# A five-engine scan of a gated delta-rule layer: the scheduler's order of four queues replaced by the written one

## Chip, cores, metric

One core of one Trainium2 chip runs the whole layer in one launch. The time is the device time of that core in microseconds; lower is better. The kernel before was timed three times.

## What is computed

One layer over 2048 latent tokens and 256 context tokens, width 1024, float32. A layer-normed, modulated input is projected to all branches at once. Branch A is a chunked gated delta rule (8 heads of 128) that runs over the tokens in both directions; branch B is a gated short convolution. Both are projected, merged by sigmoid gates, projected again and added to the input in front of a last layer norm. The core of branch A, for each head and direction, is

```
m     = tril(k_beta @ k.T * decay, -1)
t_inv = inverse(eye + m)
u, w  = t_inv @ v_beta, t_inv @ (k_beta * exp(g_cum))
qk    = (q @ k.T) * decay
v_new = u - w @ s
o     = (q * exp(g_cum)) @ s + qk @ v_new
s     = s * d + (k * exp(g_last - g_cum)).T @ v_new
```

The outputs of both directions are added, RMS-normed by head, gated, and go through `w_a`.

## The kernel before

The work has three stages. First the projections (a Strassen scheme of 512-column products, each operand split into a high and a low part). Then the scan. Then the last product with `w_out` and the layer norm.

**The scan** (function `window`, from L1164) goes over 18 chunks of 128 tokens in two directions. The directions alternate, so there are 36 visits. It is a software pipeline: iteration `i` of the loop works on four visits at once, called `v0` to `v3`.

- `v3`, the newest: `visit_load` (L97) loads `kT` and the decay exponents `gcb`; `visit_decay` (L120) makes the decay matrix (L140: eight VectorE operations, L142: one exponential, L143: one product) and the scaled query `qd` (L137, and on GpSimd L138). `gram` (L145) makes `N`, the masked product of keys, and `inv_base` (L166) begins the inverse: it negates and cuts out the diagonal blocks of 16 on ScalarE (`n32` L172, `n16` L175), finishes `n16` on VectorE (L176, L177), and then substitutes 15 times on VectorE: copy a row of the result across (L186), multiply (L187), add (L188). At the end come two masked copies on ScalarE (L191) and a transpose (L193).
- `v2`: `gram` for `QK`.
- `v1`: `inv_w16`, `inv_d16`, `inv_w32`, `inv_d32`, `inv_w64`, `inv_d64` double the inverse from blocks of 16 to 128 (small products, ScalarE evacuations in between: `w64` L276, `R` L266 and L284); `visit_load2` loads and scales `kt` on GpSimd (L118).
- `v0`, the oldest: `st_ks`, `st_v`, `st_o`, `st_u` use the state `S`: products on TensorE, `vh` on VectorE (L297), `v2` on ScalarE (L307), `S` on VectorE (L328).

In the first half of the visits the raw products of `N` and `QK` are also copied by ScalarE and stored (L161, L162). In the second half each chunk is met again from the other side: `N` and `QK` are read back instead (L152), the two directions' outputs are added (L1285), and the finished chunk is normed (`norm`: eight squares with row sums on ScalarE, L1392, twelve tiny VectorE operations that depend on each other, eight scalings, L1400) and transposed (`norm_out`, L1402). Only from iteration 17 on is `v3` such a repeated chunk.

TensorE is kept busy with **fillers** (`fillers`, L1218): the products with `w_b` and `w_a`, 1536 matmuls in eight jobs, called in portions by `dense`. A job "a" can only begin when its group of chunks has been normed. What the scan doesn't use up is done behind it, beside the preparation of `w_out` (`final`, L1417).

**The order.** Only TensorE's queue is in the order of the code:

```
        with tc.manual_schedule(engines={mybir.EngineType.PE}):
            for i in range(-3, nv):
```

VectorE, ScalarE, GpSimd and the loading queue SP are ordered by the framework's scheduler, with some evacuations marked `high_priority(100)`. An engine runs its own queue strictly in order; between engines there are only semaphores.

## Time and profile before

| | us |
|---|---|
| median of three runs | 3214.51 |
| lowest and highest run | 3212.06, 3222.6 |
| the profiled execution's own time | 3216.19 |
| its span, first to last instruction | 3214.5 |
| scan, first state product to the last fillers' start | about 1921 to 2892 of the span |
| behind it: remaining fillers, then the last stage | 2892 to 3021, 3021 to 3214.5 |

Times in the rows below count from the start of the span. PE is TensorE, PEld its weight load, DVE VectorE, ACT ScalarE, POOL GpSimd, SP the loading queue. A row `A <- B` in a list of waits says that A's engine stood idle until B released it. In a timeline, the first two numbers are start and duration; a start-to-start distance below a duration means that two operations overlap in the engine. A float32 128x128 matmul appears as two records.

### The profile page before, as it was taken

The numbers are of one execution on the slowest core, as the hardware profiler recorded it, in microseconds if no ns is written. First come the engines' busy times: TensorE is split into PE (matmuls) and PEld (weight loads), VectorE is DVE, ScalarE is ACT, GpSimd is POOL, SyncE is SP. The second block draws the span as 40 slices with busy tenths as digits, with TensorE's granted clock in tenths as the row PEclk, the third lists the DMA queues.
The fourth block names the chain that finished last, engine by engine and source line by source line (L and its number), as shares of the span: only waits on it lengthen the run. The fifth ranks groups of instructions, "written<-read, shape, count | busy, mean of one in ns | idle before, by whom it ended". The sixth has DMA issues, their size and how long they took to land.

```text
span 3214.5 us, 60268 instructions
## 1 busy us (share of the span) xinstructions
PE 2939.6 (91%) x22089; PEld 2410.3 (75%) x22089; DVE 2197.9 (68%) x5663; ACT 1518.0 (47%) x3405; POOL 1405.7 (44%) x1016
## 2 busy tenths in 40 slices
PE   7899889999998999999999978999998888896897
PEld 4678668888887777788878767888887777784776
DVE  7756746566655575565552268888889999867399
ACT  4563553333345746333344335565655666653121
POOL 3543547766567555566666401111111132315264
PEclk9999999999999999999999989999999889998999
DMA  5533763323565433132243377676687777777742
GB/s 212 142 109 86 231 214 121 102 79 113 179 192 173 134 86 100 53 86 85 79 124 109 111 282 253 220 268 222 214 299 257 242 237 267 240 264 251 243 153 102
DMA packets 405381, 557.24 MB, mean 173 GB/s; under 512 B 28244, under 2 KB 278613, under 8 KB 404060
## 3 DMA queue, kind: packets, MB, share of 16 engines
q1 hardware_dynamic: 382158, 520.77, 51.0%
q10 hardware_dynamic: 22926, 32.62, 2.8%
q8 instruction: 173, 2.83, 0.4%
q14 instruction: 124, 1.02, 0.1%
HBM read 391.66 MB, written 161.64 MB: 172 GB/s over the span
## 4 chain that ended last, share of the span: by engine, by line
PE 43%; DVE 27%; DMA 8%; issue 7%; ACT 6%; POOL 5%; SPq 1%; ACTq 0%; DVEq 0%; POOLq 0%
PE pd L758 12%; PE pd L760 12%; PE pd L759 11%; DVE rb L187 3%; DMA gcb<-gcd 3%; POOL al L342 3%; DVE rb L186 2%; DVE gcb L140 2%; DVE R L188 2%; ACT n L172 1%; DVE t L1003 1%; POOL s L744 1%; DVE S L328 1%; DVE gcb L143 1%; DVE t L1005 1%
## 5 line engine op out<-in xcount | busy, mean ns | idle before, releaser
L758 PE MATMUL pd<-bh,ah 128*128 128x512 f32 x2240 | 891.3, 398 | 10.3 <-ACT u L778 5.8
L760 PE MATMUL pd<-bh,al 128*128 128x512 f32 x2240 | 878.7, 392 | 0.0
L759 PE MATMUL pd<-bl,ah 128*128 128x512 f32 x2240 | 878.2, 392 | 0.0
L342 POOL TENSOR_TENSOR al<-s,ah 128x512 fp32r<-128x512 f32 x348 | 478.4, 1378 | 471.2 <-ACT ah L341 466.2
L342 POOL TENSOR_TENSOR al<-raw,ah 128x512 fp32r<-128x512 f32 x260 | 371.9, 1435 | 323.6 <-ACT ah L341 288.9
L758 PEld LDWEIGHTS pd<-bh,ah 128*128 128x128 f32 x2240 | 424.6, 190 | 98.9 <-issue 6.6
L760 PEld LDWEIGHTS pd<-bh,al 128*128 128x128 f32 x2240 | 424.1, 189 | 90.7 <-POOL al L342 0.2
L759 PEld LDWEIGHTS pd<-bl,ah 128*128 128x128 f32 x2240 | 424.8, 190 | 85.9
L341 ACT CAST ah<-s 128x512 fp32r<-128x512 f32 x352 | 214.6, 618 | 298.5 <-PE pd L759 261.7
L341 ACT CAST ah<-raw 128x512 fp32r<-128x512 f32 x264 | 162.3, 616 | 257.8 <-PE pd L759 166.3
L744 DVE TENSOR_TENSOR s<-s,raw 128x512 f32<-128x512 f32 x80 | 107.0, 1338 | 220.7 <-POOL s L744 220.7
L1244 PE MATMUL pf<-ah,wh 128*128 128x512 f32 x512 | 212.4, 416 | 44.4 <-DMA wh<-w_ahd 17.7
L138 POOL TENSOR_TENSOR qd<-qd,qT 128x1024 f32<-128x1024 f32 x32 | 75.7, 2367 | 393.7 <-ACT qd L137 376.7
L1248 PE MATMUL pf<-ah,wl 128*128 128x512 f32 x512 | 218.4, 427 | 2.5 <-DMA wl<-w_ald 2.5
L1246 PE MATMUL pf<-al,wh 128*128 128x512 f32 x512 | 211.0, 412 | 0.7 <-POOL al L342 0.6
L187 DVE TENSOR_TENSOR rb<-rb,n 128x56 f32<-128x56 f32 (+5 forms) x540 | 171.6, 318 | 7.1
L1244 PEld LDWEIGHTS pf<-ah,wh 128*128 128x128 f32 x512 | 101.4, 198 | 66.5 <-issue 29.4
L188 DVE TENSOR_TENSOR R<-R,rb 128x56 f32<-128x56 f32 (+5 forms) x540 | 131.3, 243 | 5.5
L1020 ACT ACTIVATE t<-t 128x512 f32<-128x512 f32 (+1 forms) x112 | 67.2, 600 | 142.2 <-DVE t L1005 142.1
L118 POOL TENSOR_TENSOR kt<-kt,kd 128x1024 f32<-128x1024 f32 x36 | 73.0, 2029 | 137.5 <-DMA kt<-kd 130.8
L315 PE MATMUL pst<-S,qd 128*128 128x128 f32 x512 | 105.5, 288 | 20.3 <-ACT v L307 12.0
L1248 PEld LDWEIGHTS pf<-ah,wl 128*128 128x128 f32 x512 | 100.9, 197 | 26.8 <-DMA wl<-w_ald 6.1
(353 smaller groups left out, 5941.3 us busy)
## 6 DMA issues: line engine op xcount, KB each, us to landing
raw<-in_w_in SPq DMA_DIRECT2D x160, 512.0 KB
kT<-kTd SPq DMA_DIRECT2D x36, 512.0 KB
gcb<-gcd SPq DMA_DIRECT2D x36, 512.0 KB
kt<-kd SPq DMA_DIRECT2D x36, 512.0 KB
vh<-vd SPq DMA_DIRECT2D x36, 512.0 KB
wh<-w_bhd SPq DMA_DIRECT2D x32, 512.0 KB
wl<-w_bld SPq DMA_DIRECT2D x32, 512.0 KB
qT<-qTd SPq DMA_DIRECT2D x32, 512.0 KB
```

Source lines behind the costliest of these rows:

```text
L187: nc.vector.tensor_tensor(out=rbv, in0=rbv, in1=bc(n16[:, :, i:i + 1], w), op=ALU.mult)
L188: nc.vector.tensor_tensor(out=R[:, :, c0:c1], in0=R[:, :, c0:c1], in1=rbv, op=ALU.add)
L315: nc.tensor.matmul(po[:, j, :], v["qd"][:, h, :], S[:, h, :], start=True, stop=False)
L341: self.nc.scalar.copy(out=hi, in_=src)
L342: (eng or self.nc.gpsimd).tensor_tensor(out=lo, in0=src, in1=hi.bitcast(F32), op=ALU.subtract)
L744: eng.tensor_tensor(out=o, in0=a, in1=b, op=op)
L758: mm(ps, hi[:, k, :], bh, start=(first and k == 0), stop=False, skip_group_check=not first)
L759: mm(ps, hi[:, k, :], bl, start=False, stop=False, skip_group_check=not first)
L760: mm(ps, lo[:, k, :], bh, start=False, stop=(last and k == 3), skip_group_check=not first)
L1244: mm(ps, wh[:, k, :], ah, start=(k == 0), stop=False)
L1246: mm(ps, wh[:, k, :], al, start=False, stop=False)
L1248: mm(ps, wl[:, k, :], ah, start=False, stop=(k == KT - 1))
```

## The change

All five queues now run in the order of the code inside the scan. To make such an order possible, functions are cut into steps:

- `visit_decay`, `inv_base` and `norm` become generators, and the loop advances them between other work (`go(dec)`, `go(sol, 2)`, `go(norms)`).
- The substitution runs by columns: the row of `n16` is copied across ahead of its use, and each step multiplies it by one column of `R` and adds. The number and the sizes of the VectorE operations are the same.
- The blocks of 64 (`inv_x16`) and the masked copies into `R` move to other places, the latter from `inv_d32` to `inv_w64`.
- Stored `N` and `QK` are requested at the start of the iteration (`gram_load`); the gates that an evacuation needs are requested ahead of the product (`ahead`); weights are requested at the start of the product before, and also across the border of two jobs; a job "a" fetches its eight inputs before it splits them. Buffers: weights 3 to 2, `yr` 3 to 8, `N` 2 to 3, `ot` 3 to 4, `mt` 1 to 2.
- From visit 0 on there are 24 fillers in an iteration of the first half and 32 in one of the second, as before, in portions of 4 and 8. Near the end there are 40 instead of 27.

The diff, cut to its core (indented by four less; lines of the old loop and of the old substitution are left out, they stand in the kernel above):

```diff
@@ -127,28 +128,35 @@
...
     nc.vector.tensor_scalar(out=t8, in0=t8, scalar1=0.0, scalar2=None, op0=ALU.min)
+    yield
     v["kd8"] = kd8 = g2.tile([P, 8], F32, name="kd8", bufs=4)
     nc.scalar.activation(out=kd8, in_=t8, func=AF.Exp)
-    nc.vector.tensor_tensor(out=kd8, in0=kd8, in1=cj, op=ALU.mult)
     v["d8"] = d8 = g2.tile([P, 8], F32, name="d8", bufs=4)
...
         nc.scalar.activation(out=qd, in_=gcb, func=AF.Exp)
-        nc.gpsimd.tensor_tensor(out=qd, in0=qd, in1=v["qT"], op=ALU.mult)
+    yield
+    nc.vector.tensor_tensor(out=kd8, in0=kd8, in1=cj, op=ALU.mult)
     for h in range(H):
...
     nc.scalar.activation(out=gcb, in_=gcb, func=AF.Exp)
+    if v["latent"]:
+        nc.gpsimd.tensor_tensor(out=qd, in0=qd, in1=v["qT"], op=ALU.mult)
+    yield
     nc.vector.tensor_tensor(out=gcb, in0=gcb, in1=bc(cj.unsqueeze(2), P), op=ALU.mult)
+def gram_load(self, v, name):
+    v[name] = self.g2.tile([P, H, P], F32, name=name, bufs=3)
+    if v["again"]:
+        self.nc.sync.dma_start(v[name], v["keep"][name])
 def gram(self, v, name, rhs):
     nc = self.nc
-    v[name] = N = self.g2.tile([P, H, P], F32, name=name, bufs=2 if name == "N" else 3)
-    kT, keep = v["kT"], v["keep"][name]
+    N, kT, keep = v[name], v["kT"], v["keep"][name]
     if v["again"]:
-        nc.sync.dma_start(N, keep)
         nc.vector.tensor_tensor(out=N, in0=N, in1=v["gcb"], op=ALU.mult)
...
@@ -170,25 +178,39 @@
...
         nc.scalar.mul(out=n32[s], in_=N[s, :, s], mul=-1.0)
+    yield
     n16 = g2.tile([P, H, 16], F32, name="n16")
...
     nc.scalar.mul(out=n16, in_=n32[:, :, 0:16], mul=self.m16[0])
+    yield
     nc.vector.scalar_tensor_tensor(out=n16, in0=n32[:, :, 16:32], scalar=self.m16[1], in1=n16, op0=ALU.mult, op1=ALU.add)
...
+    order = list(range(0, 15) if d == 0 else range(15, 0, -1))
+    left = lambda j: slice(j + 1, 16) if d == 0 else slice(0, j)
+    def row(j):
+        c = left(j)
+        w = c.stop - c.start
+        t = g2.tile([P, H * 15], F32, name="rb", bufs=3)[:, 0:H * w].rearrange("p (h c) -> p h c", c=w)
+        nc.vector.stream_shuffle(t, n16[:, :, c], [j] * 16 + [16 + j] * 16)
+        return t
+    yield
+    nxt = row(order[0])
+    for i, j in enumerate(order):
+        t, c = nxt, left(j)
+        nc.vector.tensor_tensor(out=t, in0=t, in1=bc(R[:, :, j:j + 1], c.stop - c.start), op=ALU.mult)
+        if i < 14:
+            nxt = row(order[i + 1])
+        nc.vector.tensor_tensor(out=R[:, :, c], in0=R[:, :, c], in1=t, op=ALU.add)
+        yield
     v["r32"] = r32 = g2.tile([P, H, 32], F32, name="r32")
...
         nc.scalar.mul(out=r32[:, :, 16 * hf:16 * hf + 16], in_=R, mul=self.m16[hf])
+    yield
     v["r32t"] = r32t = g2.tile([P, H, 32], F32, name="r32t")
...
@@ -219,6 +241,9 @@
...
     nc.vector.transpose(self.fl(r32t), self.fl(r32))
+def inv_x16(self, v):
+    nc, g2, r32, r32t = self.nc, self.g2, v["r32"], v["r32t"]
     v["r64"] = r64 = g2.tile([P, H, 64], F32, name="r64")
...
@@ -260,10 +285,6 @@
...
     nc.scalar.mul(out=v["r64t"][p2, :, c1], in_=dt[p2], mul=-1.0)
-    v["R"] = R = self.g2.tile([P, H, P], F32, name="R")
-    for hf in range(2):
-        c = slice(64 * hf, 64 * hf + 64)
-        nc.scalar.mul(out=R[:, :, c], in_=v["r64"], mul=self.m64[hf])
 def inv_w64(self, v):
...
@@ -274,6 +295,10 @@
...
         nc.scalar.copy(out=v["w64"][p2], in_=wp[p2])
+    v["R"] = R = self.g2.tile([P, H, P], F32, name="R")
+    for hf in range(2):
+        c = slice(64 * hf, 64 * hf + 64)
+        nc.scalar.mul(out=R[:, :, c], in_=v["r64"], mul=self.m64[hf])
 def inv_d64(self, v):
...
@@ -331,7 +356,7 @@
 def load_w(self, w, m):
-    parts = [self.wp.tile([P, KT, P], FR, name=n, bufs=3) for n in ("wh", "wl")]
+    parts = [self.wp.tile([P, KT, P], FR, name=n) for n in ("wh", "wl")]
     for t, src in zip(parts, self.w_d[w][m]):
...
@@ -1168,38 +1193,41 @@
...
+    got = {}
+    def fetch(job, k):
         if job[0] == "b":
...
+            got[k] = fe.tile([P, 512], F32, name="yr", bufs=8)
+            nc.sync.dma_start(got[k], self.ya_d[job[1]][k])
+    def feed(job, k, eng=None):
+        if job[0] == "b":
+            fetch(job, k)
+        else:
+            self.split(*cur[k], got.pop(k), eng)
+    def ahead(job, m):
         gt = fe.tile([P, 512], F32, name="gt")
...
+        if job[0] == "b":
+            nc.sync.dma_start(gt, self.gb_d[job[1]][m])
+            return gt, None
+        mt = fe.tile([P, 512], F32, name="mt")
+        for i, c in enumerate(GROUPS[job[1]][::2]):
+            sl = slice((c % 4) * P, (c % 4) * P + 256)
+            nc.sync.dma_start(gt[:, 256 * i:256 * i + 256], self.ga_d[c // 4][m][:, sl])
+            nc.sync.dma_start(mt[:, 256 * i:256 * i + 256], self.mb_d[c // 4][m][:, sl])
+        return gt, mt
+    def evac(job, m, ps, gt, mt):
         nc.vector.scalar_tensor_tensor(out=gt, in0=gt, scalar=1.0, in1=ps, op0=ALU.add, op1=ALU.mult)
...
+        if job[0] == "a":
+            (nc.vector if self.tail else nc.gpsimd).tensor_tensor(out=gt, in0=gt, in1=mt, op=ALU.add)
+        nc.sync.dma_start((self.mb_d if job[0] == "b" else self.mg_d)[job[1]][m], gt)
     jobs = JOBS
...
@@ -1226,19 +1254,29 @@
...
                 yield True
+            W = "w_b" if job[0] == "b" else "w_a"
             if not fed:
+                w = [self.load_w(W, 0)]
                 for k in range(KT):
...
+                    fetch(job, k)
+                if not self.tail:
+                    yield True
+                if job[0] == "a":
+                    for k in range(KT):
+                        feed(job, k, nc.vector if self.tail and k % 2 else None)
             fed = False
...
+                wh, wl = w.pop(0)
+                end = ahead(job, m)
+                if m < 7:
+                    w.append(self.load_w(W, m + 1))
+                elif nxt is not None and ready(nxt):
+                    fed = True
+                    w.append(self.load_w("w_b" if nxt[0] == "b" else "w_a", 0))
+                    if nxt[0] == "a":
+                        for k in range(KT):
+                            fetch(nxt, k)
                 for k in range(KT):
...
@@ -1248,13 +1286,10 @@
...
                         feed(nxt, k, nc.vector if self.tail and k % 2 else None)
-                    if k == 2 and m < 7:
-                        w = self.load_w(W, m + 1)
                     if k < KT - 1:
                         yield
-                (evac_b if job[0] == "b" else evac_a)(job[1], m, ps)
+                evac(job, m, ps, *end)
                 yield
-            w = None
     def src(d, n):
...
@@ -1277,7 +1312,7 @@
...
             hs = slice(4 * g, 4 * g + 4)
-            ot = self.g1.tile([P, 4, P], F32, name="ot", bufs=3)
+            ot = self.g1.tile([P, 4, P], F32, name="ot", bufs=4)
             if not again:
...
@@ -1302,69 +1337,112 @@
             if next(fil, None):
                 return
...
+    ET = mybir.EngineType
+    with tc.manual_schedule(engines={ET.PE, ET.DVE, ET.Activation, ET.Pool, ET.SP}):
+        norms, sol, turned = iter(()), iter(()), []
+        def go(it, n=1):
+            for _ in range(n):
+                next(it, None)
+        def turn():
+            for n, parts in turned:
+                self.norm_out(n, parts)
+                done.add(n)
+            turned.clear()
         for i in range(-3, nv):
             get = lambda k: vs[i + k] if 0 <= i + k < nv else None
             v0, v1, v2, v3 = get(0), get(1), get(2), get(3)
...
+            dec = self.visit_decay(v3) if v3 else iter(())
+            if i < -1:
+                dense(FILL(i) // 2)
             if v0:
                 self.st_ks(v0)
                 v0["o_cb"][1]()
             if v3:
                 self.visit_load(v3)
+                self.gram_load(v3, "N")
+            if v2 and v2["latent"]:
+                self.gram_load(v2, "QK")
+            go(sol, 2)
+            go(norms)
             if v1:
                 self.visit_load2(v1)
                 self.inv_w16(v1)
             if v2 and v2["latent"]:
                 self.gram(v2, "QK", v2["qT"])
...
+            if i == -1 or v2 and v2["again"] or not v2:
                 dense(8)
             if v3:
                 self.visit_load_q(v3)
+            go(sol, 2)
             if v1:
                 self.inv_d16(v1)
...
+            go(sol)
             if v0:
                 self.st_v(v0, 0)
                 self.st_v(v0, 1)
...
+            go(sol)
+            if v1:
+                self.inv_x16(v1)
+            go(dec)
+            turn()
+            if i >= -1:
+                dense(4)
+            go(sol, 2)
             if v0:
                 self.st_o(v0, 0)
+            go(sol, 2)
+            if v0:
                 self.st_u(v0, 0)
             if v1:
                 self.inv_w32(v1)
+            go(dec)
+            go(sol, 2)
             if v0:
                 self.st_o(v0, 1)
...
+            if late:
+                n, parts = late[0][0], [late.pop(0)[1:], late.pop(0)[1:]]
+                norms = self.norm(n, parts)
+                turned.append((n, parts))
+            go(norms)
+            go(sol, 2)
+            if i >= -1:
+                dense(4)
             if v0:
                 self.st_u(v0, 1)
             if v1:
+                self.inv_d32(v1)
+            go(dec)
+            go(norms)
+            go(sol, 9)
+            if i >= -1:
+                dense(8)
+            if v1:
                 self.inv_w64(v1)
...
+            go(norms)
+            go(sol, 9)
+            go(dec)
+            if i < -1:
+                dense(FILL(i) - FILL(i) // 2)
+            if v3:
+                self.gram(v3, "N", v3["kT"])
+                sol = self.inv_base(v3)
+            if i == -1 or v3 and v3["again"] or not v3:
+                dense(8)
             if v1:
                 self.inv_d64(v1)
...
+            go(sol, 2)
+            go(norms)
+            if i == -1 or not v3 or not v3["again"]:
+                dense(8)
+            go(sol)
+        go(norms, 9)
+        turn()
         return fil
 def rsqrt(self, pool, x):
@@ -1390,14 +1468,17 @@
...
             nc.scalar.activation(out=jk, in_=o[:, j, :], func=AF.Square, accum_out=ms[:, hs.start + j:hs.start + j + 1])
+        yield
     e8 = g2.tile([P, H], F32, name="e8")
...
     ms = self.rsqrt(g2, ms)
+    yield
     for hs, o in parts:
...
             nc.scalar.mul(out=o[:, j, :], in_=o[:, j, :], mul=ms[:, hs.start + j:hs.start + j + 1])
+        yield
 def norm_out(self, n, parts):
```

## Rows read from the trace of the kernel before

**Rows 1.** The page, part 1: busy time, share of the span, instructions, two engines.

```profile
PE 2939.6 (91%) x22089; PEld 2410.3 (75%) x22089; DVE 2197.9 (68%) x5663; ACT 1518.0 (47%) x3405; POOL 1405.7 (44%) x1016
```

**Rows 2.** Stretches: length, busy us of PE, PEld, DVE, ACT, POOL; PEclk, DMA.

```profile
2018.70:2364.10 345.40, 322.28 (x4900) 284.08 (x4890) 298.89 (x1265) 206.81 (x429) 60.84 (x39) 1.00 0.72 236
...
2467.40:2822.70 355.30, 302.74 (x4295) 260.72 (x4285) 325.19 (x1345) 222.91 (x626) 93.00 (x61) 0.90 0.74 245
```

**Rows 3.** The same stretches, instructions of L304 alone (PE, PEld).

```profile
2018.70:2364.10 345.40, 29.71 (x208) 25.11 (x209) 1.00 0.72 236
...
2467.40:2822.70 355.30, 28.64 (x193) 25.68 (x193) 0.90 0.74 245
```

**Rows 4.** Waits of VectorE, 2018.7 to 2364.1: total us, times, longest.

```profile
DVE n L176 <- ACT n L175: 21.8, 13, 1.7
DVE t L128 <- DMA gcb<-gcd: 12.5, 13, 3.9
```

**Rows 5.** Timeline of VectorE in one steady visit: start, duration, operation.

```profile
2281.13 0.59 DVE L297 SCALAR_TENSOR_TENSOR vh<-pst,ngam,vh 128x128 f32<-128x128 f32 x2
...
2289.34 0.21 DVE L186 STREAM_SHUFFLE rb<-R 128x48 f32<-128x48 f32 x1
...
2290.08 0.21 DVE L186 STREAM_SHUFFLE rb<-R 128x56 f32<-128x56 f32 x1
...
2295.69 2.30 DVE L187 TENSOR_TENSOR rb<-rb,n 128x96 f32<-128x96 f32 x1
...
2300.30 0.27 DVE L187 TENSOR_TENSOR rb<-rb,n 128x112 f32<-128x112 f32 x1
2300.49 0.35 DVE L140 SCALAR_TENSOR_TENSOR gcb<-gcb,gc,mask 128x128 f32<-128x128 f32 x1
...
2304.19 2.27 DVE L143 TENSOR_TENSOR gcb<-gcb,cc 128x1024 f32<-128x1024 f32 x1
```

**Rows 6.** Timeline of GpSimd in the same visit.

```profile
2295.51 2.36 POOL L138 TENSOR_TENSOR qd<-qd,qT 128x1024 f32<-128x1024 f32 x1 [16.93 <-ACT qd L137]
```

**Rows 7.** Timeline of ScalarE in the same visit.

```profile
2297.26 0.72 ACT L266 ACTIVATE R<-r,m64l 128x512 f32<-128x512 f32 x1
...
2298.62 0.58 ACT L276 COPY w<-pinv 64x512 f32<-64x512 f32 x1
2302.42 0.40 ACT L191 ACTIVATE r<-R,m16l 128x128 f32<-128x128 f32 x1 [3.22 <-DVE R L188]
...
2303.02 1.04 ACT L142 ACTIVATE gcb<-gcb 128x1024 f32<-128x1024 f32 x1
2304.09 0.59 ACT L284 ACTIVATE R<-pinv 64x512 f32<-64x512 f32 x1
...
2304.95 0.59 ACT L161 COPY zat<-gram 128x512 f32<-128x512 f32 x1
...
2305.99 0.59 ACT L161 COPY zat<-gram 128x512 f32<-128x512 f32 x1 [0.45 <-ACT zat L161]
...
2307.89 1.69 ACT L172 ACTIVATE n<-N 32x256 f32<-32x256 f32 x4 [1.31 <-DVE N L163]
2309.62 0.40 ACT L175 ACTIVATE n<-n,m16l 128x128 f32<-128x128 f32 x1
```

**Rows 8.** Groups by line, 2467.4 to 2822.7: busy us, mean ns | idle before.

```profile
L1392 ACT ACTIVATE jk<-ot 128x128 bf16<-128x128 f32 x96 | 29.4, 306 | 10.3 <-DVE ot L1285 8.4
...
L1392 ACT ACTIVATION_READ_ACCUMULATOR jk<-ot 128x1 f32 x96 | 17.9, 187 | 0.0
...
L1381 DVE SCALAR_TENSOR_TENSOR nry<-nrt,nry 128x8 f32<-128x8 f32 x36 | 6.8, 189 | 0.0
```

**Rows 9.** Waits of VectorE, 2467.4 to 2822.7: total us, times, longest.

```profile
DVE t L128 <- DMA gcb<-gcd: 7.0, 6, 3.2
DVE n L176 <- ACT n L175: 6.0, 8, 1.7
```

**Rows 10.** Waits of TensorE, 2892 to 3021: total us, times, longest.

```profile
PE pf L1244 <- DMA wh<-w_ahd: 17.7, 4, 11.6
```

More of the change, by code (lines that the diff above doesn't have):

```diff
@@ L180, in inv_base @@
         nc.gpsimd.tensor_copy(out=R, in_=rows(self.i16))
-        rb = g2.tile([P, H, 16], F32, name="rb")
-        for i in (range(15, 0, -1) if d == 0 else range(0, 15)):
-            c0, c1 = (i, 16) if d == 0 else (0, i + 1)
-            w = c1 - c0
-            rbv = rb.rearrange("p h c -> p (h c)")[:, 0:H * w].rearrange("p (h c) -> p h c", c=w)
-            nc.vector.stream_shuffle(rbv, R[:, :, c0:c1], [i] * 16 + [16 + i] * 16)
-            nc.vector.tensor_tensor(out=rbv, in0=rbv, in1=bc(n16[:, :, i:i + 1], w), op=ALU.mult)
-            nc.vector.tensor_tensor(out=R[:, :, c0:c1], in0=R[:, :, c0:c1], in1=rbv, op=ALU.add)
+        order = list(range(0, 15) if d == 0 else range(15, 0, -1))
[15 more added lines that the diff above has]
+            yield
         v["r32"] = r32 = g2.tile([P, H, 32], F32, name="r32")
@@ L1210, in window @@
         for k in range(KT):
-            feed(jobs[0], k)
+            fetch(jobs[0], k)
         w0 = self.load_w("w_b", 0)
@@ L1238, in fillers @@
                     ps = pd.tile([P, 512], F32, name="pf")
-                    wh, wl = w
-                    if m == 7:
-                        fed = nxt is not None and ready(nxt)
+                    wh, wl = w.pop(0)
[8 more added lines that the diff above has]
+                                fetch(nxt, k)
                     for k in range(KT):
@@ L1308, in window @@
                 v0, v1, v2, v3 = get(0), get(1), get(2), get(3)
-                nd = FILL(i)
-                part = [nd * 4 // 26, nd * 4 // 26, nd * 10 // 26]
-                part = part + [nd - sum(part)] if i >= -1 else [0, 0, 0, nd]
+                dec = self.visit_decay(v3) if v3 else iter(())
+                if i < -1:
+                    dense(FILL(i) // 2)
                 if v0:
@@ L1321, in window @@
                     self.gram(v2, "QK", v2["qT"])
-                if v2 and v2["again"]:
+                if i == -1 or v2 and v2["again"] or not v2:
                     dense(8)
@@ L1346, in window @@
                 if v1:
-                    self.inv_w64(v1)
-                dense(part[2])
+                    self.inv_d32(v1)
[5 more added lines that the diff above has]
+                if v1:
+                    self.inv_w64(v1)
+                go(norms)
[8 more added lines that the diff above has]
+                    dense(8)
                 if v1:
                     self.inv_d64(v1)
-                if i == -3:
-                    dense(part[3])
-                if v3:
-                    self.gram(v3, "N", v3["kT"])
-                    self.inv_base(v3)
-                if i > -3:
-                    dense(part[3])
-                while late and late[0][0] != v0["n"]:
-                    n, parts = late[0][0], [late.pop(0)[1:], late.pop(0)[1:]]
-                    self.norm(n, parts)
-                    self.norm_out(n, parts)
-                    done.add(n)
-            for n, hs, o in late:
-                if hs.start == 0:
-                    self.norm(n, [x[1:] for x in late if x[0] == n])
-                    self.norm_out(n, [x[1:] for x in late if x[0] == n])
-                    done.add(n)
+                go(sol, 2)
[5 more added lines that the diff above has]
+            turn()
             return fil
```

41 lines of the change are left out of this document (2 added, 39 removed).

## The prediction

> **What bounds the kernel now.** Over the whole span TensorE looks like the limit: busy 91%, VectorE 68% [rows 1]. That is an average over three stages, and the change touches the scan, so I cut the scan into stretches. The records of L304, 16 in a visit, count the visits: 208 make 13 visits in 345.40 us, 26.57 us each; 193 make 12 in 355.30 us, 29.61 each [rows 3]. In the first of these stretches both chunks are new, in the second they are repeated. VectorE is busy 298.89 us of the first (87%) and 325.19 of the second (92%), TensorE 322.28 (93%) and 302.74 (85%) [rows 2]. TensorE's busy time holds its waits inside a pipelined stream, so I asked who waits. In the first stretch VectorE waits for just two things: 21.8 us for ScalarE's `n16` and 12.5 for the load of `gcb`, both 13 times, so 1.68 and 0.96 us in every visit [rows 4]. Everything else of its 26.57 us is work, or work held up. **The scan goes at VectorE's pace**: nearly every microsecond that its queue stands still is lost. The question for the change is therefore what VectorE's queue stands waiting for once its order is written by hand.
>
> The timeline of one steady visit shows three prices. A step of the substitution that runs alone takes 0.74 us (shuffle to shuffle, 2289.34 to 2290.08), three operations of which each needs the one before, so 0.25 each [rows 5]. An operation that needs nothing of the one ahead starts after 0.19 us although that one lasts 0.27 (L187, then L140 at 2300.49) [rows 5]. And a product of two SBUF operands stands still while GpSimd multiplies: L187 takes 2.30 us, against the 0.27 of a larger one, from just behind the start of GpSimd's 2.36 us multiply of `qd` [rows 5, 6].
>
> **The change, part by part, in a visit of the first stretch.**
>
> *Removed.* `n16` is now asked for in steps, and `gcb` is used later in the iteration than it is loaded (two evacuations and two substitution steps lie between), so I take both old waits away: 2.64 us.
>
> *The columns.* The shuffle no longer depends on the last add. Two dependent operations remain in a step, 0.50 instead of 0.74 us. That helps only where the step ran alone, since the scheduler had already put other work between: about 5 of 15 in the visit shown. Saving 1.2 us; bounds 0 (all were covered) and 3.7 (none was). The Trainium skill speaks against even this: "VectorE: DVE Perf Modes", section "Rules for kernel authors", says that chained VectorE operations drain in any case, so that only their number counts. By it this saving is 0 and the sum 16 us higher; the overlap in the row above speaks for the saving.
>
> *The new waits.* I followed each queue through one iteration. Call E the moment when VectorE has done its eight operations of L140. Behind it in ScalarE's written order stand: the exponential 1.04, two copies of `r32` 0.40 each, `w64` 0.58, two copies into `R` 0.72 each, two copies and stores of `N`'s raw products, 1.04 from start to start, the evacuation into `R` 0.59, four operations for `n32` 1.69, `n16` 0.40 [rows 7]. Sum 8.6 us. VectorE needs two of these. After one more substitution step (0.5) it waits for `r32`, until E + 1.84: 1.3 us. Then come the transpose (an estimate of 0.3), the product with `cc` and the two products of `N`; before, these last took from 2304.19 to 2307.89, 3.70 us, with part of L143's 2.27 a hold by GpSimd's `kt` [rows 5, 7]. So VectorE is done at E + 5.8, or E + 4.7 without that hold, and waits for `n16` until E + 8.6: 2.8 to 3.9 us, I take 3.3, between them, as the hold may come at another place. **Queued behind this wait are the eight operations on `vh` of the next visit**, though their product has been there for long, and TensorE's `st_v` waits for them. Before, two of them (0.59 us [rows 5]) had slipped ahead of the wait; and before, `w64` and the copies into `R` ran ahead of the exponential, at 2297 to 2299 [rows 7], where now they delay `n32`.
>
> *The holds by GpSimd* stay: its multiplies wait for the same inputs, and most of VectorE's work between is of the kind that they hold. Cost 0; if the cover of that argument goes, up to 2.0 less (2.30 against 0.27) [rows 5] where a multiply falls into one of the new waits.
>
> Net: -2.64 - 1.2 + 1.3 + 3.3 = +0.8 us, times 13: **+10 us**. Bounds: with the full saving and the short wait -2.2, but TensorE's 24.8 busy us in a visit (322.28 by 13 [rows 2]) stop that at -1.8, so -23 us; with no saving and the long wait +2.6, +33 us.
>
> **In a visit of the second stretch** there is more in the chain. Old waits go: 7.0 and 6.0 us in 12 visits [rows 9], 1.1 in one. The second four squares of the norm now stand between the exponential and `r32` on ScalarE: 0.306 + 0.187 each [rows 8], 1.97 us. `r32` is there at E + 1.04 + 1.97 + 0.8 = 3.8, and VectorE, ready at 0.5, waits 3.3. The raw products are not copied here, so ScalarE is ready for `n32` when `N` is; but `n32` and `n16` follow it, 1.69 + 0.40 [rows 7], 2.1 us in which VectorE has only an evacuation now and then; I take 1.7. The twelve tiny operations of the norm, 0.189 each [rows 8], now run as one chain, 2.3 us; mixed with the substitution they cost about half. So +1.2, bounds 0 and 2.3. The substitution's saving is nothing here, as the scheduler had filled its gaps with the norm. Net -1.1 + 3.3 + 1.7 + 1.2 = +5.1 us, times 12: **+61 us**. Bounds: without the norm's term and with half of the `r32` wait +2.2, +27; with everything +6.6, +79.
>
> **The rest.** *Prefetch.* In the fillers behind the scan TensorE waits 17.7 us in four places for weights [rows 10], the longest (11.6) at the border of two jobs, which the change crosses with a load one product ahead. Not all comes back, as the transfers are the same: -8 us, bounds 0 and -17.7. *The three visits of the entry, the first four, the four between the stretches, the last three:* same counts of work, the waits above partly; the 40 fillers near the end leave fewer behind. 0, bounds -15 and +15. *More buffers, `gram_load`, `ahead`:* 0, since no wait for `N`, `QK` or a gate is among VectorE's in these stretches [rows 4, 9]; the loads are covered by the iteration. *SP in order:* a store now holds the loads written behind it until VectorE has evacuated; 0 as long as the next weights are already there (a rival below).
>
> **Sum.** 3216.2 (the profiled execution's own time) + 10 + 61 - 8 = 3279 us. That execution lies 1.7 us above the median of the runs, so 3278.
>
> **Rivals.**
>
> *1. Faster: the chain on ScalarE doesn't show, TensorE becomes the bound.* Place: between L140's last operation and the next `vh`. If GpSimd's multiplies fall into the waits (2.0 less), and the columns save 3.7, then 4.6 us of new waits are paid for, and both stretches fall to TensorE's busy time, 24.8 and 25.2 us in a visit [rows 2]. That is -23 and -53, with the prefetch -84: 3132 us; half way 3174. For it: in the first stretch the net is small against its bounds, and portions of 4 and 8 fillers are placed where TensorE would wait. Against it: ScalarE's order is what it is written to be, and the second stretch needs over 5 us more. It decides where E to the next `vh` is under 5 us. Chance 0.31.
>
> *2. No change:* half of the second stretch's cost, paid by prefetch and the columns; 3205 to 3225. Chance 0.09.
>
> *3. Slower still, by SP.* Place: the border of two products, where the store waits for VectorE, then two buffers of weights and `kT` and `gcb` of the next visit wait behind it. A wait for weights costs 17.7 / 4 = 4.4 us behind the scan [rows 10]. The scan crosses some 47 such borders; at half of them +103: 3380. Against it: weights come a whole product ahead. Chance 0.08.
>
> **How the numbers follow.** The forecast itself has 0.52, with a range of its own of 3225 to 3343 (both stretches at their bounds). Rival 1 adds the lower side, and I cut it at 3125, a little beyond its full price; above 3345 only rival 3 is left out. Some 0.2 lies outside. Faster by over 0.3% (about 10 us, what three runs can tell from no change) 0.31, within 0.09, slower 0.52 + 0.08 = 0.60.
>
> **What would show it.** Right: VectorE waits for ScalarE's `n16` 3 us in every visit of the first stretch, its transposes (`r32t` from `r32`) 1 to 3 us; the first stretch at 27 to 28 us a visit, the second at 33 to 36; VectorE's busy share of both lower, near 80%; the weights' wait at the job border gone; single operations of VectorE still held over 1 us by GpSimd. Wrong: VectorE without waits over 1 us and a first stretch under 26 us (rival 1), or waits of TensorE for `wh` and of VectorE for `gcb` in front (rival 3).

## The result: 12.5% slower, and the profile after

| | before | after |
|---|---|---|
| median of the runs, us | 3213.48 (3212.06 to 3222.6, 4 runs) | 3619.26 (3615.66 to 3620.05, 4 runs) |
| ratio | | 1.1254, 95% interval [1.1231, 1.1276] |
| span of the profiled execution | 3214.5 | 3613.9 |
| first 13 visits / repeated 12 visits, us each | 26.57 / 29.61 | 29.90 / 49.39 |
| in front of the scan / from the last visit's L304 (L329 after) to the end | 1921.5 / 347.0 | 1941.3 / 370.2 |

The direction was forecast, the size was not: 3278 was predicted, and 3345 was the end of the range. Of the 399 us, the repeated visits hold 237, the first stretch 43, and the entry, the border visits, the end of the scan and what lies in front of it and behind it 119.

The page of after, part 1 (against [rows 1]):

```profile
PE 3033.2 (84%) x22089; PEld 2499.0 (69%) x22089; DVE 2237.2 (62%) x5658; ACT 1516.8 (42%) x3405; POOL 1395.4 (39%) x1021
```

The two stretches of after, the same visits as in [rows 2] and with the same columns, then the records of L329 (L304 before), which count 13 and 12 visits as in [rows 3]:

```profile
2058.10:2446.80 388.70, 339.19 (x4900) 300.83 (x4888) 307.30 (x1277) 207.35 (x430) 58.46 (x39) 0.93 0.60 215
2578.80:3171.50 592.70, 337.12 (x4289) 298.04 (x4281) 349.46 (x1348) 223.42 (x628) 87.73 (x63) 0.74 0.45 159
...
2058.10:2446.80 388.70, 26.68 (x208) 24.20 (x208) 0.93 0.60 215
2578.80:3171.50 592.70, 29.54 (x193) 26.96 (x193) 0.74 0.45 159
```

VectorE's work hardly grew (325.19 to 349.46 us in the repeated visits), but its share fell from 92% to 59%: it stands. For whom, the waits tell; first stretch of after (against [rows 4]):

```profile
DVE n L186 <- ACT n L184: 20.3, 13, 1.8
DVE r32t L215 <- ACT r L212: 18.4, 13, 1.4
DVE t L129 <- DMA gcb<-gcd: 16.0, 11, 3.0
DVE N L171 <- ACT zat L169: 15.4, 26, 1.0
```

The repeated visits of after (against [rows 9]):

```profile
DVE QK L160 <- DMA QK<-kqd: 71.7, 12, 12.0
DVE zat L1494 <- DMA zat<-zad: 71.0, 16, 10.1
DVE r32t L215 <- ACT r L212: 36.1, 12, 3.0
DVE n L186 <- ACT n L184: 33.8, 12, 11.4
```

The two lines for ScalarE are the forecast. The two for loads, 143 us of VectorE alone, are not in it at all. What held those loads stands in the waits of SP's queue. Over the scan (1840 to 3250), and for the first stretch alone, the longest row is:

```profile
SPq L1230 <- DVE gt L1227: 378.4, 24, 23.2
...
SPq L1230 <- DVE gt L1227: 202.0, 11, 19.1
```

L1230 is the store of a finished dense product. A queue that stands long is not yet a loss: SP stands 202.0 us at these stores in the first stretch, and of the loads behind them VectorE waits there for `gcb` alone, 16.0 us. The repeated visits are another matter:

```profile
SPq L1495 <- DVE zat L1494: 126.7, 15, 14.3
SPq L1230 <- POOL R L190: 102.6, 5, 22.4
SPq L102 <- PE pst L320: 86.1, 7, 19.4
SPq L1230 <- POOL gt L1229: 51.4, 6, 17.4
```

Here SP stands at two stores (L1495 a part of the normed chunk; L1230, which in a job "a" waits for an addition on GpSimd, and that for VectorE's evacuation; the row that names GpSimd's `R` L190 means the operation next to such an addition in GpSimd's queue) and at `kT`, whose buffer comes free with the product of `kT` and the state, L320. SP's timeline over one repeated visit of after shows what is behind them:

```profile
2625.07 0.50 SPq L1490 DMA_DIRECT2D zat<-zad  x1
2637.48 0.37 SPq L1495 DMA_DIRECT2D yad<-zat  x1
2637.89 0.50 SPq L1490 DMA_DIRECT2D zat<-zad  x1
2641.92 0.37 SPq L1495 DMA_DIRECT2D yad<-zat  x1
2642.51 0.33 SPq L1230 DMA_DIRECT2D mbd<-gt  x1
...
2644.06 4.89 SPq L1311 DMA_DIRECT2D op<-od  x2
2663.27 0.32 SPq L102 DMA_DIRECT2D kT<-kTd  x1
2663.68 0.39 SPq L104 DMA_DIRECT2D gcb<-gcd  x1
2664.12 0.42 SPq L153 DMA_DIRECT2D N<-kkd  x1
2664.59 0.42 SPq L153 DMA_DIRECT2D QK<-kqd  x1
```

And VectorE's timeline of the same visit:

```profile
2636.70 0.75 DVE L1494 SCALAR_TENSOR_TENSOR zat<-gram,cvT,zat 128x512 f32<-128x512 f32 x1
2641.14 0.75 DVE L1494 SCALAR_TENSOR_TENSOR zat<-gram,cvT,zat 128x512 f32<-128x512 f32 x1 [3.69 <-DMA zat<-zad]
...
2671.59 1.23 DVE L160 TENSOR_TENSOR QK<-QK,gcb 128x1024 f32<-128x1024 f32 x1 [1.94 <-DMA QK<-kqd]
```

Read them together. VectorE ends the first half of the norm's output at 2637.45; the store goes at 2637.48; only behind it may SP ask for the second `zat` (2637.89), and VectorE waits 3.69 us for it. The store of L1230 goes at once in this visit. Then SP stands at `kT`: from the end of the `op` loads (2648.95) to 2663.27 it issues nothing, 14.3 us, until TensorE has come to L320 at the head of the next iteration. `N` and `QK` go right behind `kT`; `QK` is asked for 7.0 us before VectorE starts on it, in the same iteration, and VectorE has waited 1.94 us by then. **A circle**: the loads stand behind a store, or behind a load, that waits for VectorE's work or for TensorE's next iteration, and VectorE waits for the loads.

### The profile page after: what moved, and what is told of

Same layout as the page of the kernel before. It is cut to its first block, busy times and chain, and to the rows that moved or that the text cites. A ratio compares the mean times of both kernels' runs of the same rounds, so it can differ in the third digit from the quotient of the medians.

```text
span 3613.9 us, 60210 instructions
## 1 busy us (share of the span) xinstructions
PE 3033.2 (84%) x22089; PEld 2499.0 (69%) x22089; DVE 2237.2 (62%) x5658; ACT 1516.8 (42%) x3405; POOL 1395.4 (39%) x1021
## 5 line engine op out<-in xcount | busy, mean ns | idle before, releaser
L367 POOL TENSOR_TENSOR al<-raw,ah 128x512 fp32r<-128x512 f32 x260 | 370.2, 1428 | 320.7 <-ACT ah L366 285.2
L1282 PE MATMUL pf<-ah,wh 128*128 128x512 f32 x512 | 227.1, 444 | 49.3 <-DMA wh<-w_bhd 17.2
L340 PE MATMUL pst<-S,qd 128*128 128x128 f32 x512 | 122.1, 327 | 151.3 <-DVE ot L1320 139.4
L1286 PE MATMUL pf<-ah,wl 128*128 128x512 f32 x512 | 230.2, 450 | 18.2 <-DMA wl<-w_ald 16.7
L1284 PE MATMUL pf<-al,wh 128*128 128x512 f32 x512 | 223.7, 437 | 2.7 <-POOL al L367 2.6
L340 PEld LDWEIGHTS pst<-S,qd 128*128 128x128 f32 x512 | 97.4, 232 | 157.4 <-DVE ot L1320 141.5
L208 DVE TENSOR_TENSOR R<-R,rb 128x120 f32<-128x120 f32 (+4 forms) x540 | 189.3, 350 | 1.2
L205 DVE TENSOR_TENSOR rb<-rb,R 128x120 f32<-128x120 f32 (+4 forms) x540 | 166.8, 309 | 14.2
L1282 PEld LDWEIGHTS pf<-ah,wh 128*128 128x128 f32 x512 | 110.0, 215 | 74.0 <-issue 30.4
L308 PE MATMUL pinv<-r,w 64*64 64x64 f32 x576 | 57.2, 272 | 113.2 <-ACT w L297 113.2
```

Of the source, the lines that this page charges most:

```text
L205: nc.vector.tensor_tensor(out=t, in0=t, in1=bc(R[:, :, j:j + 1], c.stop - c.start), op=ALU.mult)
L208: nc.vector.tensor_tensor(out=R[:, :, c], in0=R[:, :, c], in1=t, op=ALU.add)
L340: nc.tensor.matmul(po[:, j, :], v["qd"][:, h, :], S[:, h, :], start=True, stop=False)
L367: (eng or self.nc.gpsimd).tensor_tensor(out=lo, in0=src, in1=hi.bitcast(F32), op=ALU.subtract)
L1282: mm(ps, wh[:, k, :], ah, start=(k == 0), stop=False)
L1284: mm(ps, wh[:, k, :], al, start=False, stop=False)
```

## Experiments

Each starts from the changed kernel unless another is named. Where no interval is given the time is of a single execution, beside the kernel before on the same chip (3211 to 3220); the runs of the kernel before differ by up to 0.4%, 3208.89 to 3222.6 us, so a difference of some 15 us between two single executions says little.

**1. Which queue's order costs.** The set of hand-ordered queues is cut; all else stays.

```diff
-        with tc.manual_schedule(engines={ET.PE, ET.DVE, ET.Activation, ET.Pool, ET.SP}):
+        with tc.manual_schedule(engines={ET.PE, ET.DVE, ET.Activation, ET.Pool}):
```

> The kernel after, but SP's queue is ordered by the scheduler again; the other four stay in the written order. Theory SP (the stores that wait for VectorE, and the load of kT that waits for a product, hold QK, the gates za and gcb behind them): VectorE's waits for QK (6.0 us a visit) and za (5.9) in the second stretch and for gcb (1.2) in the first go away, 49.4 falls to 37 or 38 us and 29.9 to 28.7, the time to 3400 to 3450. Theory ORDER (the coarse order of VectorE and ScalarE sets the pace, loads are only what is waited for last): the same time is then waited for ScalarE and TensorE, and the run stays above 3550.

Measured 3321.52: **298 us come back with SP's order alone**, more than theory SP gave. The visits take 27.87 and 35.57 us; the prediction's were 27.4 and 34.7. With `engines={ET.PE}`:

> The kernel after with all its steps, columns, loads ahead and buffers, but only TensorE's queue in the written order, as in the kernel before. If the written order of four queues is the whole cost, about 3200 (3180 to 3220: the loads ahead and the columns may give up to 30 us). If the new places of the parts or the smaller weight buffers cost by themselves, 3250 or more.

3209.8: the whole loss is in the written order of the four queues. With `{ET.PE, ET.DVE, ET.Pool}`:

> The kernel after with SP's and ScalarE's queues ordered by the scheduler; TensorE, VectorE and GpSimd stay in the written order. Theory ORDER, ScalarE's chain: against the run with SP alone free, VectorE's waits for r32 (1.2 and 2.6 us a visit) and n16 (1.7 and 2.0) shrink by half or more and TensorE's for w64 (2.1 and 4.0) with them: first stretch 26 to 26.7 us a visit, second 31 to 33, 3240 to 3270. Rival, VectorE's own coarse order is the cost (each chain alone, holds by GpSimd uncovered): under 20 us gained, over 3300.

3287.0, 26.53 and 34.48 us a visit. ScalarE's order beside SP's is worth 34 us, less than the theory said and more than the rival. The first stretch is then where it was before (26.57). The largest wait that is left of the repeated visits comes from VectorE's own queue; TensorE's first wait there:

```profile
PE pst L329 <- DVE vh L322: 70.2, 12, 13.1
```

That is `vh` held behind VectorE's other work, 5.85 us a visit.

**2. The loads earlier.** `QK` is asked for at the end of the iteration before, the norm's inputs where the norm begins.

```diff
-                if v2 and v2["latent"]:
-                    self.gram_load(v2, "QK")
...
                     sol = self.inv_base(v3)
+                    if v3["latent"]:
+                        self.gram_load(v3, "QK")
...
-                    turned.append((n, parts))
+                    turned.append((n, parts, self.norm_load(n, parts)))
...
```

`norm_load` holds the two loads that stood in `norm_out`.

> The kernel after, all five queues written, but QK is requested at the end of the iteration before and both halves of za where the norm begins, not where they are used. Theory SP: VectorE's waits for QK and za, 11.9 us in a visit of the second stretch, fall under 2: about 120 us there and 20 in the visits around it, 3470. Theory ORDER: under 40 us gained, over 3570.

3433.57, 186 us less, more than theory SP gave; the repeated visits fall from 49.39 to 37.87 us, and `QK` and `zat` are gone from VectorE's first waits:

```profile
DVE r32t L215 <- ACT r L212: 36.1, 12, 3.0
DVE n L186 <- ACT n L184: 33.9, 12, 11.6
DVE t L129 <- DMA gcb<-gcd: 15.1, 4, 5.1
```

**3. `kT` behind the loads that need no state.** Its load moves from the head of `visit_load` to behind `visit_load2`.

```diff
-        v["kT"] = self.gk.tile([P, H, P], F32, name="kT", bufs=3)
-        nc.sync.dma_start(v["kT"], src["kT"])
...
                     self.visit_load2(v1)
+                if v3:
+                    self.visit_load_k(v3)
```

> The kernel after, all five queues written, but the load of kT, whose buffer comes free only with the first product of the iteration, is written behind the loads of gcb, N, QK, kt and vh instead of ahead of them. If the place of kT in SP's queue is what makes QK and gcb late: VectorE's wait for QK falls from 6.0 to under 2 us a visit of the second stretch, for gcb from 1.2 to under 0.5 in the first, together 60 to 80 us, 3540. If the stores ahead of it hold SP just as long, under 20 us.

3553.1, 66 us less, as expected. But VectorE's wait for `QK` fell from 5.98 to 3.65 us a visit only, not under 2; the stores, which are still in front, probably hold it (experiment 4 bears that out). The wait for `gcb` in the first stretch fell from 16.0 to 2.4 us.

**4. The store later, and all three repairs.**

```diff
-            nc.sync.dma_start((self.mb_d if job[0] == "b" else self.mg_d)[job[1]][m], gt)
+            owed.append(((self.mb_d if job[0] == "b" else self.mg_d)[job[1]][m], gt))
...
                     for k in range(KT):
+                        if k == 3:
+                            pay()
```

> All five queues written; the store of a finished dense product (L1230) is issued three eighths into the next product instead of right behind its evacuation. In the changed kernel SP stands 378 us in 24 places of the scan at these stores. Theory (loads that would have been free to go stand behind the stores): 40 to 120 us off, 3500 to 3580 us. Rival (the loads behind would have waited for their own buffers anyway): within 25 us of 3619.

3484.04, 135 us less, more than expected, for moving each 256 KB store by less than half a product. In the repeated visits VectorE's wait for `QK` falls from 71.7 to 26.1 us and that for `zat` from 71.0 to 50.4: the store held both. Together with 2 and 3:

> All five queues written, with all three repairs of SP's order together: QK and the norm's inputs requested early, kT behind the loads that need no state, the store later. Theory (these three places are SP's share): near the version whose SP order was free (3321.52), 3325 to 3360 us; second stretch 35 to 36.5 us a visit, first 27.5 to 28.5. Rival (SP's loss is spread over many places, or ScalarE's queue carries it too): over 3385 us.

3338.55, **281 us less, with all five queues still written**, inside the expected band. The parts alone sum to 387; they free the same loads twice. These are the waits of VectorE in this version, first stretch, then repeated visits, with the windows of both:

```profile
DVE n L188 <- ACT n L186: 22.5, 13, 1.9
DVE r32t L217 <- ACT r L214: 18.4, 13, 1.4
DVE N L173 <- ACT zat L171: 15.8, 26, 1.0
...
DVE r32t L217 <- ACT r L214: 36.1, 12, 3.0
DVE n L188 <- ACT n L186: 24.5, 12, 2.2
...
2035.90:2403.90 368.00, 330.71 (x4891) 295.10 (x4889) 300.71 (x1273) 207.47 (x430) 58.64 (x39) 0.95 0.62 225
2515.90:2940.80 424.90, 316.63 (x4287) 279.24 (x4281) 343.37 (x1339) 224.71 (x628) 90.99 (x63) 0.86 0.62 215
```

Not one wait for a load is left in front. This is the kernel that the prediction described; it lies 60 us above the 3278 predicted, and the section on the prediction says where.

**5. What is left then.** VectorE's order to the scheduler, on experiment 2 and on the three repairs:

```diff
-        with tc.manual_schedule(engines={ET.PE, ET.DVE, ET.Activation, ET.Pool, ET.SP}):
+        with tc.manual_schedule(engines={ET.PE, ET.Activation, ET.Pool, ET.SP}):
```

> The version with the early loads (3433.57 us with all five queues written), with VectorE's order left to the scheduler; TensorE, ScalarE, GpSimd and SP as written. Theory (with the loads mended, what is left is VectorE's own order: in-order waits for n16 and r32, and vh held behind the norm): second stretch from 37.9 to 31 to 33 us a visit, first from 29.7 to 27 to 28, 3290 to 3340 us. Rival (SP's and ScalarE's orders carry the rest): over 3390 us, second stretch over 36.

3306.89, 127 us under experiment 2; the second stretch at 31.81 us a visit is as expected, the first at 28.69 above.

> The version with the three repairs of SP's order and VectorE's order left to the scheduler; TensorE, ScalarE, GpSimd and SP as written. Theory (SP's three places and VectorE's own order are the whole loss): 3210 to 3240 us, within 1% of the kernel before; the second stretch at 29 to 30.5 us a visit. Rival (the written orders of ScalarE and GpSimd cost something by themselves): over 3265 us.

3265.44: just the rival's side. All of the gain is in the repeated visits, 35.41 to 31.35 us; the first stretch, 28.31 before and 28.81 now, gains nothing. TensorE's first wait in its repeated visits names the next queue:

```profile
PE pinv L310 <- ACT w L299: 37.1, 11, 4.6
```

That is `w64`, written behind ScalarE's long operations. With ScalarE free too (`{ET.PE, ET.Pool, ET.SP}`):

> The three repairs of SP's order, with both VectorE's and ScalarE's orders left to the scheduler; TensorE, GpSimd and SP as written. Theory (what is left at 3265.44, 1.6% above the kernel before, is ScalarE's written order: TensorE waits 3.1 us a visit of the second stretch for w64, whose copy stands behind the exponential): 3205 to 3230 us, that wait under 0.5 us. Rival (SP's written order, though mended, or GpSimd's): over 3250 us.

3231.72, 2 us above the expected band; that wait is down to 1.1 us. But the gain does not come from there: the repeated visits fall only from 31.35 to 30.74 us, 7 of the 34 us, and the first stretch, which that row does not cover, from 28.81 to 26.42, 31 us. So the loss, in steps taken in this order: SP's three places 281 us, VectorE's order 73, ScalarE's 34, what the orders of SP and GpSimd still cost 20, down to 3211.8 (experiment 7). In another order the steps have other sizes (VectorE's is worth 127 where only experiment 2 is done), and GpSimd's queue was never freed alone.

**6. ScalarE's chain shortened.** `r32`'s copies ahead of the exponential and of the norm's squares, the copies into `R` (now `inv_R`, cut out of `inv_w64`) behind `inv_d32`; once alone, once with the early loads.

```diff
...
                     self.inv_d32(v1)
-                go(dec)
-                go(norms)
-                go(sol, 9)
+                go(sol, 2)
+                if v1:
+                    self.inv_R(v1)
+                go(dec)
+                go(sol, 9)
+                go(norms)
...
```

> The kernel after with another order of ScalarE at the end of an iteration: the last step of the substitution and the copies r32 ahead of the decay's exponential and of the norm's second squares, and the copies into R back behind inv_d32, ahead of it as well. Theory ORDER, ScalarE's chain: VectorE's wait for r32 (1.4 us a visit in the first stretch, 3.0 in the second) goes, and its wait for n16 shrinks in the first: 1.5 to 2 us a visit in the first stretch (28.2), 3 in the second (46.4), together 80 to 100 us, 3520 to 3540. Theory SP: what is gained is waited for the next load, under 30 us in the second stretch, 3570 or more.

3567.37, 52 us less instead of some 90: between the two theories. The first stretch gains its 1.5 us a visit (28.38), the second 1.4 instead of 3 (48.0). The wait for `r32` is gone there, but the squares are late in its place:

```profile
DVE ms L1481 <- ACT jk L1476: 25.9, 12, 2.3
```

> The kernel after with both edits: QK and za requested early, and r32 and R ahead of the exponential and the squares on ScalarE. If the two costs lie one behind the other, their gains add: 186 and 52 us, 3380. Theory SP-covers (ScalarE's chain is hidden while VectorE waits for loads in the second stretch, where the second edit gave only 1.4 us a visit): with the loads early the second edit is worth its 3 us there, so 20 to 30 us more, 3350 to 3360. If ScalarE's chain just moves on, 3410 or more.

3395.85: 38 us under experiment 2, between the sum of the gains (52) and a chain that just moves on (24 at most). Much of the chain is passed on, from one consumer to the next.

**7. The substitution by columns, and a version that beats both.** Columns alone in the kernel before (the loop of the change's diff in place of the old one):

> The kernel BEFORE with the substitution by columns and nothing else changed; VectorE's order is the scheduler's. From the timeline (a step alone 0.74 us by rows; 0.53 by columns in the kernel after): if steps that ran alone are shortened, 1.2 us a visit, 36 visits, 43 us faster at most, 3170 to 3195. If VectorE's operations cost what they cost whatever they wait for, or the scheduler had covered the chain, within 10 us of before.

3246.55, ratio 1.009 [1.0066, 1.0114]: slower, against both expectations. The scheduler made another order of the whole visit; VectorE's first wait of the first stretch is one that cost 0.11 us a visit before (that row first):

```profile
DVE N L163 <- ACT zat L161: 1.4, 4, 0.3
...
DVE N L163 <- ACT zat L161: 40.5, 26, 4.9
```

In the changed code with TensorE's queue alone written:

> The changed code with TensorE's queue alone written, timed against the kernel before (one look gave 3209.8 against 3219.67). Theory (the written order of the other four queues makes the whole loss, the rest of the change is neutral): ratio between 0.994 and 1.001, about 3200 to 3217 us. Rival (the rest of the change gains by itself, and the written order costs more than 400 us): under 0.99, under 3185 us.

3211.8, ratio 0.9979 [0.9966, 0.9991]: a little faster than before, as the theory had it. The same with the old loop over rows:

> The same with the substitution by rows again, as in the kernel before; everything else of the change stays, TensorE's queue alone is written. Theory (a step by columns is shorter, and that shows where the step runs alone): 5 to 20 us slower than with columns, 3215 to 3230 us. Rival (columns give the scheduler nothing or cost, as where they alone were put into the kernel before and the time rose 30 us): equal, or faster by up to 30 us, 3180 to 3210 us.

3259.85, ratio 1.0139 [1.0122, 1.0156]. Here the columns are worth 48 us, more than twice what the theory gave. So that the rest of the change is neutral holds only with the columns in it: with rows the same code is 1.4% slower than the kernel before. The same two stretches, first by columns, then by rows:

```profile
2012.10:2367.30 355.20, 328.79 (x4890) 292.45 (x4888) 290.88 (x1284) 207.40 (x431) 65.48 (x39) 0.96 0.67 233
2465.10:2812.30 347.20, 296.21 (x4286) 255.80 (x4281) 330.87 (x1340) 221.39 (x624) 97.60 (x61) 0.92 0.72 249
...
2015.00:2381.90 366.90, 329.53 (x4895) 291.25 (x4889) 312.47 (x1275) 206.69 (x430) 65.41 (x39) 0.96 0.66 227
2493.70:2866.80 373.10, 299.31 (x4289) 259.09 (x4281) 349.01 (x1329) 220.42 (x617) 91.66 (x62) 0.89 0.73 243
```

VectorE is busy 21.6 and 18.1 us less by columns, at about the same number of operations. Part of the 48 us is that, part the scheduler's new order: the two can't be told apart while it orders the queues, and the sign in the kernel before was the other one. Last, a third buffer for `gcb`:

```diff
-        self.gb = self.pool(es, "gb", 2)
+        self.gb = self.pool(es, "gb", 3)
```

> TensorE's queue alone written, and a third buffer for gcb. In the version without it VectorE waits 2.17 us a visit of the first stretch for the load of gcb, and the issues of that load wait for VectorE's last use of an old buffer. Theory (the buffer is what makes it late): that wait under 0.5 us, first stretch from 27.1 to 25.3 to 26 us a visit, 15 to 24 us off, 3185 to 3200 us. Rival (the load then waits for its place in SP's order, or another wait takes over): within 6 us of the version without it.

3210.59, ratio 0.9975 [0.9963, 0.9987]: the rival. VectorE still waits 27.6 us for `gcb` in the first stretch (29.6 without the third buffer).

## Why the prediction was wrong, point by point

**What bounds.** Right. VectorE's standing time in the first stretch went from 46.5 to 81.4 us (length less busy, [rows 2] and the windows above): 35 of the 43 us. In the repeated visits it went from 30.1 to 243.2.

**The failed step: the two terms that were put at 0, "SP in order" and "More buffers, `gram_load`, `ahead`", the latter "since no wait for `N`, `QK` or a gate is among VectorE's" and "the loads are covered by the iteration".** The rows of before show no such wait, but in SP's timeline of before the scheduler asks for both halves of the norm's input at once, and stores both at once later:

```profile
2582.64 0.91 SPq L1409 DMA_DIRECT2D zat<-zad  x2
...
2611.56 0.98 SPq L1414 DMA_DIRECT2D yad<-zat  x2
```

A wait that this order avoids can't be bounded by its absence. Nor does the iteration cover the loads: that holds for `N`, which is used near the end of the iteration in which it is asked for, but `QK` is used early in its own, and each half of the norm's input where it is asked for. The prediction says that each queue was followed through one iteration, but for SP no such list is in it: that would have shown `kT`, which waits for a state product, in front of `gcb`, `N` and `QK`, the store of L1230 in front of all of them, and the second `zat` load behind the store of the first half. Those moved DMAs were costed at nothing; they cost 281 us (experiment 4), or 298 with SP's whole order given back (experiment 1). Rival 3 had the mechanism, stores that hold loads, down to `kT` and `gcb`, but priced it by four waits for weights, at 103 us, and gave it 0.08. `QK` and the norm's input, the two that cost most, are not in it.

**The forecast mechanism, ScalarE's chain.** Right in kind, as the version with SP's order mended shows. `r32`: 18.4 / 13 = 1.42 us a visit in the first stretch (1.3 predicted) and 36.1 / 12 = 3.01 in the second (3.3). `n16`: 1.73 (3.3 predicted) and 2.04 (1.7). The first is short, and no longer than the 1.68 of the kernel before [rows 4]; but one step earlier stands a wait on the same chain that the prediction did not have: VectorE's two products of `N` wait for ScalarE's raw copies, 15.8 / 13 = 1.22. The stretches cost +22.6 and +69.6 us in that version; the sum had +10 and +61, with a bound of 79 for the second. That the first came out within its bound of 33 is in part luck: the wait that was missing (1.2) and the saving by columns that did not show (below) stand against an `n16` that was 1.6 too long.

**Old waits removed, -2.64.** Half right. `n16` stayed as a wait of its own, as forecast; `gcb` did not go in the changed kernel (16.0 us against 12.5 in [rows 4]) and is no longer among VectorE's first waits once SP does not hold its load.

**The columns.** The single step is as predicted: VectorE's timeline of one visit of after has 2331.17 to 2331.69, 0.52 us, where 0.50 was predicted against 0.74 [rows 5]:

```profile
2331.17 0.23 DVE L205 TENSOR_TENSOR rb<-rb,R 128x64 f32<-128x64 f32 x1
2331.32 0.01 DVE L198 LOAD_MASK_SELECT rb<-n  x1
2331.32 0.21 DVE L198 STREAM_SHUFFLE rb<-n 128x56 f32<-128x56 f32 x1
2331.45 0.21 DVE L208 TENSOR_TENSOR R<-R,rb 128x64 f32<-128x64 f32 x1
2331.69 0.22 DVE L205 TENSOR_TENSOR rb<-rb,R 128x56 f32<-128x56 f32 x1
```

The Trainium skill's rule that only the number of operations counts ("VectorE: DVE Perf Modes", section "Rules for kernel authors") is not borne out for this step, in which one of three operations no longer hangs on the one before it: three operations as before, 0.22 us less. But the term, -1.2 us a visit, does not show where VectorE's order is written: with SP's order mended VectorE is busy 300.71 us in the first stretch, against 298.89 before [rows 2]. Where the scheduler orders VectorE it is 21.6 us less by columns (experiment 7).

**The norm's chain and the holds.** Twelve tiny operations, about 0.2 us apart, in one chain, as predicted; with SP's order mended VectorE is busy 18.2 us longer in the repeated visits than before, 1.5 a visit, where the term was 1.2. That the norm makes all of it is not shown. Holds by GpSimd stay: a L208 of 24 columns at 2648.73 of after takes 2.29 us.

**Prefetch, -8.** Wrong: 0. The stretch behind the scan takes 130.4 us (129.0 before); the wait only moved from `wh` [rows 10] to `wl`, in TensorE's waits there:

```profile
PE pf L1286 <- DMA wl<-w_ald: 16.7, 11, 5.5
```

**Entry, border visits and end, 0 with 15 either way.** Wrong. With what lies in front of the scan and behind it they cost 119 us in the changed kernel and still 30 with SP's order mended (122.3 of span less 22.6 and 69.6). They have the same chain as the other visits and should have had its price: in that version VectorE waits 7.3 us for `r32` and 7.6 for `n16` in the four visits between the stretches, where before it waited 2.8 for `n16` and 3.0 for `gcb`. So of the 60 us by which that version lies above the prediction, 13 and 9 are the stretches' and 38 these visits' and the prefetch's.

**The range.** Its upper end, 3343, is the sum of the upper bounds (33, 79, 0 and 15 on 3216.2). The lower end, 3225, is not the sum of the lower ones, which give 3188; this does not bear on the miss, which lies above.

**The rivals.** Rival 1 fell: with VectorE's order written, no version came under the kernel before. Only with VectorE, ScalarE, GpSimd and SP all scheduled is there a gain, of 0.2%.

## What to carry to other kernels

Before a loading queue is put in written order, list its issues over one iteration with what each waits for: a store or a load into a reused buffer holds every load behind it, and where the engine it waits for needs one of those loads, the delay comes round again each iteration. Ask for loads a whole iteration ahead, and issue a store well behind its evacuation. That a wait is missing from a profile says nothing of the same resource in another order: cost a moved DMA by its new place in the queue.

## What the runs showed of the hardware

Two engines that only read one PSUM tile take turns here. In the changed kernel VectorE's product of `N` waits for ScalarE's copy of the same tile, all 26 times in 13 visits, 15.4 / 26 = 0.59 us each, about the length of the copy itself [rows 7]. The Trainium skill says why such a dependency is made ("PSUM — Partial Sum Buffer", section "PSUM bank collisions raise a hardware error": two engines on one bank at once raise an error, two readers included); the trace agrees with the wait, and no run here shows the error.

TensorE's products run longer behind the waits of others. In the repeated visits of after its mean granted clock, made up of stretches at full and at half speed, is 0.74 of full speed where it is busy 57% of the time, against 0.90 at 85% before [rows 2], and the same products keep it busy 337.12 us instead of 302.74; with SP's order mended it is 0.86 and 316.63 us. The dense products, which follow each other closely, have no part in it (L1282 430 ns in the mean, L1244 before 430); the scan's products that come behind a wait, or soon behind it, do: the query with the state 357 ns after (L340), 292 before (L315), `kT` with the state 411 after (L320), 333 before (L295). How much of this lengthens a visit is not shown.
